# Each expert bias matmul queued behind the last product before it

## The chip, the cores and the metric

One core of one Trainium2 chip runs the program. The metric is the device time of one execution in microseconds. The kernel before took 1867.7 us (median of three executions, 1866.82 to 1869.79). The profile comes from one further execution.

## The reference

A decoder block on 512 tokens of width 1024, all float32: a mixer (a state-space branch and a pooling branch, gated), then a mixture of experts, then a final norm. What matters here is the mixture. Each token goes to 4 of 32 experts, and an expert computes

```
gu = xblk @ w_gu[e] + b_gu[e]            # 1024 -> 2048
act = glu * sigmoid(1.702 * glu) * (lin + 1)   # after clamping
out = act @ w_down[e] + b_down[e]        # 1024 -> 1024
y += out * gate                          # added to the token's row
```

## The kernel before

The mixer runs until about 713 us of the span, the mixture of experts from there to about 1850 us, and the last norm ends the program. The experts are ranked by their token counts. Those with up to 64 tokens take a *half* form: 64 rows, plain float32 products, the weights used as they were loaded. The others take a *full* form: up to 128 rows, each 1024-column piece of weights split into a high and a low part by one ScalarE (ACT) copy (L117) and one VectorE (DVE) subtraction (L118), and three products in place of one. `order_of_ranks` (L62) sets the order: one full expert, two half ones, then full and half in turn with the largest expert in the middle (it has a second block of rows), at last five full ones and two half ones.

The loop at L1351 goes over the experts. In its step u it first calls `up` for expert u (L1366), then `down` for expert u-1 (L1388). Both first call `biases`: one matmul a PSUM bank, which opens the bank's sum (`start=True`) with a row that a selector (`sel` or `wide`) picks from the bias table `bt`. `up` opens four banks of the tag "mm" for a full expert and two for a half one, `down` two or one of the tag "ss"; each tag has four banks. Then `products` adds to these banks for k = 0 to 7: L1111 to L1113 in the full form (96 matmuls in `up`, 48 in `down`), L1106 in the half form (in the trace 64 and 32 instructions on 64 columns of the array, two groups of 64 rows each). After each load of weights, hooks run: in `down` of expert u-1 they are the activation of expert u (`act_rows` from L1145, `act_turn` with transposes at L1066 from L1154), the selector of expert u+1 (`select`, L1268, GpSimd (POOL): L1273 and for half experts L1276), and the transposes that turn the rows of expert u+1 (L1082). `prep` of expert u+2 (slots, L1038 and L1039, gather L1052, gates L1059) hangs on the first k of `up`. After `down`, `send` scales the result (L1171 on ACT, L1172 on POOL) and adds it to its rows by a scattered DMA (L1175).

The order in which an engine issues is not the program's order: a planner lays the instructions out, engine by engine, when the kernel is built, by data dependences and by the times at which it thinks operands are ready. An instruction that it thinks ready can be put ahead of earlier ones of the program. On the chip each engine then follows its list. Weights are loaded on the SP queue (L771), 1 MB each, twelve an expert, into a ring of buffers, each load as soon as its buffer has been read.

Of the kernel before, what the change touches and what calls it, by code (L numbers as in the profile page):

```python
# [1 line left out]

# [1 line left out]

# [64 lines left out]
def hybrid_block(ctx: ExitStack, tc: tile.TileContext, cst, cols, rows, xt, xf, wad0, wada, bada,  # L69
                 wx, wz, wdt, wu, wg, wso, wpl, wpo, wo, wr, ball, wgu, wdn, out):  # L70
    nc = tc.nc
    V, S, G, TE, SP = nc.vector, nc.scalar, nc.gpsimd, nc.tensor, nc.sync
# [9 lines left out]
    def T_(tag, cols_, dt=F32, parts=P):  # L82
        if tag in shared:
            o = shared[tag]
            return Z[0:parts, o:o + cols_]
        uid[0] += 1
        return sb.tile([parts, cols_], dt, tag=tag, name=f"{tag}_{uid[0]}")

    def bank(tag="mm"):
        uid[0] += 1  # L90
        return pm.tile([P, 512], F32, tag=tag, name=f"{tag}_{uid[0]}")
# [21 lines left out]
    def tt(out_, in0, in1, op):  # L113
        V.tensor_tensor(out_, in0, in1, op=op)
# [369 lines left out]
    for jj in range(4):  # L484
        whi, wlo = load_split(wpo[jj])
        for i in range(2):
            j = jj * 2 + i
            ps = bank("mm")
# [254 lines left out]
    def weights(e):  # L743
        def of(w, lo_, hi_):
            return w[e, lo_:hi_, :] if isinstance(e, int) else w[bass.ds(e, 1), lo_:hi_, :].squeeze(0)

        return dict(wu=lambda k: of(wgu, k * P, (k + 1) * P), got={},
                    wd=lambda c: of(wdn, c * 256, (c + 1) * 256).rearrange("(k p) d -> p k d", p=P))
# [5 lines left out]
    def weights_of(u):  # L754
        if u not in wts:
            wts[u] = weights(order[u] if u < FIXED else
                             SP.value_load(rk["eidi"][0:1, order[u]:order[u] + 1], min_val=0, max_val=NE - 1))
        return wts[u]
# [87 lines left out]
    for n in range(2):  # L846
# [6 lines left out]
        for b in range(NB):  # L853
            ps = bank("mm")
# [163 lines left out]
    def op_of(rot, half):  # L1018
        return Op(rot(512) if half else rot(2048, F32R), half)
# [5 lines left out]
    def slots(i, pos, n_, xe):  # L1025
        half = n_ <= 64
        s4 = T_(("a2", "wrt")[i % 2 if i != "x" else 0], 4 * P, BF16)
        for b in range(NB):
            o = s4[:, b * P:(b + 1) * P]
            if half:  # L1030
                V.tensor_scalar(o.rearrange("p (h m) -> p h m", h=2), iota1[:, 0:64].unsqueeze(1).to_broadcast([P, 2, 64]),
                                pos(b), None, op0=ALU.is_equal)
            else:
                V.tensor_scalar(o, iota1, pos(b), None, op0=ALU.is_equal)
        ps = bank("ss")
        for b in range(NB):
            sb_ = s4[:, b * P:(b + 1) * P]
            TE.matmul(ps[:, 0:2], sb_, tokc[:, 0:2], start=b == 0, stop=False)  # L1038
            TE.matmul(ps[:, 0:2], sb_, tokc[:, 2 + 2 * b:4 + 2 * b], start=False, stop=b == NB - 1)  # L1039
        n = i if i == "x" else i % 6  # L1040
        st = dict(s4=s4, ps=ps, xe=xe, n=n, half=half, rows=P if half else min(n_, P))
        ix_ = T_(f"ixs_{n}", 2)
        stt(ix_[:, 0:1], ps[:, 1:2], cs[:, C_NP:C_NP + 1], cs[:, C_P5:C_P5 + 1], ALU.mult, ALU.add)
        tt(ix_[:, 0:1], ps[:, 0:1], ix_[:, 0:1], ALU.add)
        if half:
            stt(ix_[:, 1:2], ix_[:, 0:1], 2.0, cs[:, C_H:C_H + 1], ALU.mult, ALU.add)
        idx = T_(f"idx_{n}", 1, I32)
        V.tensor_copy(idx, ix_[:, 1:2] if half else ix_[:, 0:1])
        src, lim, xe = (h_d2, 2 * T - 1, xe[:, 0:512]) if half else (h_d, T - 1, xe)
        if i != 0:  # L1050
            n_ = st["rows"]
            G.indirect_dma_start(xe[0:n_, :], None, src, bass.IndirectOffsetOnAxis(ap=idx[0:n_, :], axis=0), bounds_check=lim, oob_is_err=False)  # L1052
        st.update(idx=idx, ixf=ix_[:, 0:1])
        return st

    def slot_gates(st, gv, ps=None):
        ps = ps or st["ps"]
        for b in range(NB):
            TE.matmul(ps[:, 2:5], st["s4"][:, b * P:(b + 1) * P], gv(b), start=b == 0, stop=b == NB - 1)  # L1059
        st["gate"] = T_(f"gate_{st['n']}", 1)  # L1060
        V.tensor_reduce(st["gate"], ps[:, 2:5], axis=AX.X, op=ALU.add)
# [27 lines left out]
    def rows_of(ps, n):  # L1089
        return ps[n // 2][n % 2 * 64:n % 2 * 64 + 64, :]  # L1090


    def biases(x, ps, sel, n0):
        for n, p in enumerate(ps):
            if x.half:
                c = n0 // 2 + n
                TE.matmul(p, sel["wide"], bt[:, c * 512:(c + 1) * 512], start=True, stop=False)
            else:
                h, c = (n0 + n) % 2, (n0 + n) // 2
                TE.matmul(p, sel["cols"][:, h:h + 1].to_broadcast([P, P]), bt[:, c * 512:(c + 1) * 512], start=True, stop=False)  # L1100

    def products(x, ps, k, hl, o, n0=0):
        stop = k == KD - 1
        if x.half:
            for i in range(2):
                TE.matmul(rows_of(ps, n0 + i), x.c[k], hl[:, o + i * 512:o + (i + 1) * 512], start=False, stop=stop)  # L1106
            return
        hi, lo = hl
        for i in range(2):
            p, h, l = ps[n0 + i], hi[i], lo[i]  # L1110
            TE.matmul(p, x.h[k], h, start=False, stop=False)  # L1111
            TE.matmul(p, x.h[k], l, start=False, stop=False)  # L1112
            TE.matmul(p, x.l[k], h, start=False, stop=stop)  # L1113

    def pieces(r, full):
        for o in (0, 1024):
# [46 lines left out]
    def acts(ps, aT):  # L1163
        h = len(ps) // 2
        return [lambda n=n: act_turn(act_rows(ps[n], ps[n + h]), aT, n) for n in range(h)]
# [54 lines left out]
    def sel_halves(out_, e):  # L1220
        stt(out_, cs[:, C_PM:C_PM + 2], e, cs[:, C_HM:C_HM + 2], ALU.is_equal, ALU.mult)


    def tabled(u):
        ev = SP.value_load(tab["eui"][0:1, u], min_val=0, max_val=NE - 1)
        ec, ub, eo, pu, gvu, gvf = (T_(n, c, d) for n, c, d in (
            ("ec", 2, F32), ("ub", 1, F32), ("eo", NE, F32), ("pu", 4, F32), ("gvu", 12, BF16), ("gvf", 12, F32)))
        V.tensor_copy(ec[:, 0:1], tab["euf"][:, u])
        V.tensor_copy(ec[:, 1:2], tab["ruf"][:, u])
        V.tensor_copy(ub, tab["ubase"][:, u])  # L1230
        V.tensor_scalar(eo, i32c, ec[:, 1:2], None, op0=ALU.is_equal)
        gvt = T_("q16", 512)
        pv = gvt[:, 0:P].rearrange("p (b e) -> p b e", b=NB)
        tt(pv, rk["pos"], eo.unsqueeze(1).to_broadcast([P, NB, NE]), ALU.mult)
        V.tensor_reduce(pu, pv, axis=AX.X, op=ALU.add)
        V.tensor_scalar(pu, pu, ub, None, op0=ALU.subtract)
        gvx = gvt[:, P:P + 384].rearrange("p (b c e) -> p b c e", b=NB, c=3)
        for b in range(NB):
            tt(gvx[:, b], GVv[:, b].rearrange("p e c -> p c e"), eo.unsqueeze(1).to_broadcast([P, 3, NE]), ALU.mult)
        V.tensor_reduce(gvf.rearrange("p (b c) -> p b c", c=3), gvx, axis=AX.X, op=ALU.add)  # L1240
        V.tensor_copy(gvu, gvf)
        eT = T_("eT", 2, F32R)
        sel_halves(eT, ec[:, 0:1])
        return dict(pos=lambda b: pu[:, b:b + 1], gv=lambda b: gvu[:, b * 3:(b + 1) * 3], sel=dict(cols=eT), **weights(ev))
# [12 lines left out]
    def sel_of(u):  # L1257
        if u < FIXED:
            return dict(cols=sel0[:, 2 * u:2 * u + 2])
        return dict(cols=sels[u % 2], wide=wides[u % 2])  # L1260
# [90 lines left out]
    for u in range(NE + 1):  # L1351
        hooks = {}
        if u < NE:
            w, sel = weights_of(u), sel_of(u)
# [71 lines left out]

    nov = nc.values_load(tab["novi"][0:1, 0:1], min_val=0, max_val=OVER - 1)
    with tc.For_i(0, nov, 1) as i:
        w = tabled(bass.ds(i, 1))
        xet = T_("S6", 2048)  # L1430
        G.memset(xet, 0.0)
        st = slots(6, w["pos"], P, xet[:, 0:D])
        slot_gates(st, w["gv"])
        x = turn(st, x_rot)
        aT = op_of(a_rot, False)
        for f in acts(up([x], w["sel"], w, {})[0], aT):
            f()
        part = spread(down([aT], w["sel"], w, {})[0], st)
        for b, n in sums:
            ps = bank("mm")  # L1440
            sT, cr = part[n]
            for r in range(2):
                TE.matmul(ps, sT[:, b * P:(b + 1) * P], cr[r], start=r == 0, stop=r == 1)
            tn = t0[b][:, n * 512:(n + 1) * 512]
            tt(tn, tn, ps, ALU.add)
        for b in range(NB):
            norm(b, o_rot(1024), [t0[b][:, n * 512:(n + 1) * 512] for n in range(2)])
# [85 lines left out]
```

## Time and profile before

| What | Value |
|---|---|
| median of three executions | 1867.7 us |
| the profiled execution's own time | 1870.85 us |
| its span in the profile | 1869.1 us |
| TensorE busy | 1788.1 us, 96% |
| DVE busy | 1213.9 us, 65% |
| ACT busy | 947.0 us, 51% |
| DMA over the span | mean 282 GB/s |

The median leaves out nothing that the profile has: the profiled execution is 3.15 us above it, and 1.75 us of its own time lie outside the span. Times in the profile are counted from the start of the span. A matmul's duration includes its way through the array, and successive ones overlap, so what a matmul costs is read from one start to the next.

### The profile page before, as it was taken

The numbers are of one execution on the slowest core, as the hardware profiler recorded it, in microseconds if no ns is written. First come the engines' busy times: TensorE is split into PE (matmuls) and PEld (weight loads), VectorE is DVE, ScalarE is ACT, GpSimd is POOL, SyncE is SP. The second block draws the span as 40 slices with busy tenths as digits, with TensorE's granted clock in tenths as the row PEclk, the third lists the DMA queues.
The fourth block names the chain that finished last, engine by engine and source line by source line (L and its number), as shares of the span: only waits on it lengthen the run. The fifth ranks groups of instructions, "written<-read, shape, count | busy, mean of one in ns | idle before, by whom it ended". The sixth has DMA issues, their size and how long they took to land. (4 is left out here: it accounts for less than half of the span.)

```text
span 1869.1 us, 23339 instructions
## 1 busy us (share of the span) xinstructions
PE 1788.1 (96%) x8353; PEld 1165.1 (62%) x8353; DVE 1213.9 (65%) x1803; ACT 947.0 (51%) x1458; POOL 220.0 (12%) x214
## 2 busy tenths in 40 slices
PE   6999999999999999999999999999999999999995
PEld 3787687867768777456456455455564565677741
DVE  5888685857574548657557566375675585799933
ACT  4433545536362346346455455264555455577822
POOL 0000000010100002121111111121112111211111
PEclk9999999999999999999999999999999999999998
DMA  8265233352443458999999998789999999989894
GB/s 349 76 251 221 90 135 113 113 134 93 124 130 136 178 218 296 371 402 400 388 373 402 380 366 326 305 309 373 382 402 377 380 403 364 397 327 341 316 365 191
DMA packets 102728, 527.81 MB, mean 282 GB/s; under 512 B 11737, under 2 KB 12377, under 8 KB 60368
## 3 DMA queue, kind: packets, MB, share of 16 engines
q1 hardware_dynamic: 90544, 498.14, 68.8%
q0 software_dynamic: 11184, 25.50, 6.4%
q10 hardware_dynamic: 880, 2.64, 0.4%
q8 instruction: 67, 1.10, 0.2%
q14 instruction: 53, 0.43, 0.1%
HBM read 502.89 MB, written 25.77 MB: 283 GB/s over the span
## 5 line engine op out<-in xcount | busy, mean ns | idle before, releaser
L118 DVE TENSOR_TENSOR wl<-r,wh 128x1024 fp32r<-128x1024 f32 x246 | 303.6, 1260 | 109.4 <-ACT wh L117 100.2
L117 ACT ACTIVATE wh<-r 128x1024 fp32r<-128x1024 f32 x246 | 253.9, 1057 | 136.3 <-PE mm L266 56.2
L118 DVE TENSOR_TENSOR wl<-S,wh 128x1024 fp32r<-128x1024 f32 x186 | 229.8, 1271 | 34.3 <-ACT wh L117 34.1
L1112 PE MATMUL mm<-wl,S 128*128 128x512 f32 x540 | 217.3, 402 | 9.7 <-DVE wl L118 9.0
L1113 PE MATMUL mm<-wh,S 128*128 128x512 f32 x540 | 214.5, 397 | 0.0
L117 ACT ACTIVATE wh<-S 128x1024 fp32r<-128x1024 f32 x186 | 189.5, 1055 | 47.5 <-PE mm L1113 34.9
L265 PE MATMUL mm<-S,wh 128*128 128x512 f32 x512 | 207.9, 407 | 4.0 <-ACT S L117 4.0
L267 PE MATMUL mm<-S,wl 128*128 128x512 f32 x512 | 206.3, 403 | 1.5 <-DVE wl L118 1.5
L266 PE MATMUL mm<-S,wh 128*128 128x512 f32 x512 | 206.5, 403 | 0.0
L1111 PE MATMUL mm<-wh,S 128*128 128x512 f32 x540 | 177.7, 402 | 8.0 <-ACT wh L117 8.0
L1147 DVE TENSOR_SCALAR q<-mm 128x512 f32<-128x512 f32 x49 | 32.9, 687 | 181.8 <-PE mm L1106 153.1
L1148 ACT ACTIVATE q<-q 128x512 f32<-128x512 f32 x50 | 31.3, 632 | 218.0 <-DVE q L1147 217.8
L1112 PEld LDWEIGHTS mm<-wl,S 128*128 128x128 f32 x540 | 102.2, 189 | 47.6 <-DVE wl L118 17.0
L1111 PEld LDWEIGHTS mm<-wh,S 128*128 128x128 f32 x540 | 100.6, 188 | 48.7 <-ACT wh L117 16.3
L265 PEld LDWEIGHTS mm<-S,wh 128*128 128x128 f32 x512 | 97.2, 190 | 33.0 <-issue 7.1
L1113 PEld LDWEIGHTS mm<-wh,S 128*128 128x128 f32 x540 | 102.4, 190 | 21.5
L267 PEld LDWEIGHTS mm<-S,wl 128*128 128x128 f32 x512 | 97.0, 190 | 29.7 <-issue 6.4
L266 PEld LDWEIGHTS mm<-S,wh 128*128 128x128 f32 x512 | 97.3, 190 | 26.9 <-issue 4.2
L1112 PE MATMUL ss<-wl,S 128*128 128x512 f32 x240 | 97.1, 405 | 1.9 <-DVE wl L118 1.5
L1106 PE MATMUL mm<-S,S 128*64 128x512 f32 x408 | 96.2, 596 | 0.0
L1172 POOL TENSOR_TENSOR y<-y,q 128x512 f32<-128x512 f32 x47 | 67.7, 1453 | 237.9 <-ACT y L1171 237.2
L1113 PE MATMUL ss<-wh,S 128*128 128x512 f32 x240 | 95.5, 398 | 0.0
(499 smaller groups left out, 3101.2 us busy)
## 6 DMA issues: line engine op xcount, KB each, us to landing
S<-in_wgu SPq DMA_DIRECT2D x113, 1024.0 KB, 9.6
r<-in_wgu SPq DMA_DIRECT2D x97, 1024.0 KB, 8.4
S<-in_wdn SPq DMA_DIRECT2D x61, 1024.0 KB, 11.7
r<-in_wdn SPq DMA_DIRECT2D x44, 1024.0 KB, 13.2
bc<-in_wgu SPq DMA_DIRECT2D x23, 1024.0 KB, 10.3
Z<-in_wgu SPq DMA_DIRECT2D x23, 1024.0 KB, 10.0
r<-in_wada SPq DMA_DIRECT2D x16, 1024.0 KB, 6.7
r<-in_wx SPq DMA_DIRECT2D x12, 1024.0 KB, 6.1
```

The lines of the kernel that those rows point to most:

```text
L117: S.activation(hi, src, AF.Copy)
L118: V.tensor_tensor(lo, src, hi.bitcast(F32), op=ALU.subtract)
L265: TE.matmul(ps, a, hh(k), start=k == 0, stop=False)
L266: TE.matmul(ps, a, hl(k), start=False, stop=False)
L267: TE.matmul(ps, b, hh(k), start=False, stop=k == KD - 1)
L1106: TE.matmul(rows_of(ps, n0 + i), x.c[k], hl[:, o + i * 512:o + (i + 1) * 512], start=False, stop=stop)
L1111: TE.matmul(p, x.h[k], h, start=False, stop=False)
L1112: TE.matmul(p, x.h[k], l, start=False, stop=False)
L1113: TE.matmul(p, x.l[k], h, start=False, stop=stop)
L1147: V.tensor_scalar(g, pg, LIM, None, op0=ALU.min)
L1148: S.activation(t, g, AF.Tanh, scale=ALPHA / 2)
L1172: G.tensor_tensor(yn, yn, gaf2[0] if half else gaf[n], op=ALU.mult)
```

## The change

`products` remembers its last matmul in `lastp`. `biases` issues its matmuls under `tc.issue_after`, which queues them behind that matmul in TensorE's order; it adds no wait for a result. The matmul remembered is the last one that stands before the biases in the program: for `up` of expert u+1 it is the last product of `down` of expert u-1, and for `down` of expert u-1 it is the last product of `up` of expert u. The first expert's `up` has none. The loop at the end for experts with more tokens than their room forgets it first.

```
+    lastp = []
+
     def biases(x, ps, sel, n0):
+        with tc.issue_after(lastp[0]) if lastp else nullcontext():
+            bias_rows(x, ps, sel, n0)
+
+    def bias_rows(x, ps, sel, n0):
         for n, p in enumerate(ps):
...
         if x.half:
             for i in range(2):
-                TE.matmul(rows_of(ps, n0 + i), x.c[k], hl[:, o + i * 512:o + (i + 1) * 512], start=False, stop=stop)
+                lastp[:] = [TE.matmul(rows_of(ps, n0 + i), x.c[k], hl[:, o + i * 512:o + (i + 1) * 512], start=False, stop=stop).ins]
             return
...
-            TE.matmul(p, x.l[k], h, start=False, stop=stop)
+            lastp[:] = [TE.matmul(p, x.l[k], h, start=False, stop=stop).ins]
...
     with tc.For_i(0, nov, 1) as i:
+        lastp.clear()
         w = tabled(bass.ds(i, 1))
```

## Rows read from the trace of the kernel before

**Rows 1.** The page's first part: busy us, share of the span, instructions.
```profile
PE 1788.1 (96%) x8353; PEld 1165.1 (62%) x8353; DVE 1213.9 (65%) x1803; ACT 947.0 (51%) x1458; POOL 220.0 (12%) x214
```

**Rows 2.** Stretches: length; PE, PEld, DVE, ACT, POOL busy; PEclk, DMA share, GB/s.
```profile
923.20:991.10 67.90, 65.15 (x301) 37.93 (x299) 42.23 (x58) 36.03 (x51) 10.82 (x10) 1.00 0.98 382
991.10:1060.40 69.30, 66.56 (x299) 39.07 (x297) 42.34 (x58) 36.02 (x51) 10.82 (x10) 0.98 0.99 382
1684.40:1724.60 40.20, 38.33 (x179) 29.65 (x178) 37.36 (x42) 31.50 (x40) 8.40 (x5) 1.00 0.89 331
```

**Rows 3.** TensorE's waits at full heads, 923 to 991 us: total, times, longest.
```profile
PE mm L1112 <- DVE wl L118: 0.8, 1, 0.8
PE mm L1111 <- ACT wh L117: 0.7, 2, 0.5
```

**Rows 4.** Timeline around the start of a half expert's up: start, us, instruction.
```profile
901.54 0.72 PE L1100 MATMUL ss<-bt,sel 128*128 128x512 f32 x2
902.10 0.27 PE L1066 MATMUL mm<-cst,S 128*128 128x128 f32 x1
...
905.05 0.48 PE L1100 MATMUL mm<-bt,sel 128*128 128x512 f32 x1
905.46 1.94 PE L1106 MATMUL mm<-S,S 128*64 128x512 f32 x8
...
907.43 0.49 PE L1100 MATMUL mm<-bt,sel 128*128 128x512 f32 x1
...
907.85 5.37 PE L1106 MATMUL mm<-r,S 128*64 128x512 f32 x24
```

**Rows 5.** Timeline of TensorE where the next full expert's products begin to overlap.
```profile
958.30 1.07 PE L1106 MATMUL ss<-S,r 128*64 128x512 f32 x2
959.30 0.50 PE L1112 MATMUL mm<-wl,S 128*128 128x512 f32 x1
...
960.41 1.93 PE L1106 MATMUL ss<-S,r 128*64 128x512 f32 x6
962.28 0.55 PE L1066 MATMUL mm<-cst,S 128*128 128x128 f32 x3
```

**Rows 6.** Timeline at the end of a half expert's up.
```profile
920.02 0.50 PE L1100 MATMUL mm<-bt,sel 128*128 128x512 f32 x1
920.88 0.50 PE L1100 MATMUL mm<-bt,sel 128*128 128x512 f32 x1 [0.36 <-DVE q L1149]
922.21 0.55 PE L1066 MATMUL ss<-cst,q 128*128 128x128 f32 x3 [0.82 <-DVE q L111]
```

**Rows 7.** Timeline of all engines at the head of a full expert's up.
```profile
934.42 1.27 ACT L1171 ACTIVATE y<-ss,gate 128x512 f32<-128x512 f32 x2 [2.73 <-PE ss L1113]
934.64 0.62 PE L1111 MATMUL mm<-wh,S 128*128 128x512 f32 x2
...
936.67 3.34 DVE L118 TENSOR_TENSOR wl<-r,wh 128x1024 fp32r<-128x1024 f32 x2 [2.83 <-ACT wh L117]
...
938.93 0.50 PE L1112 MATMUL mm<-wl,S 128*128 128x512 f32 x1 [0.80 <-DVE wl L118]
```

**Rows 8.** One bias of a half expert's down among full products.
```profile
926.38 0.48 PE L1097 MATMUL ss<-bt,sw 128*128 128x512 f32 x1
926.69 0.40 PE L1112 MATMUL ss<-wl,S 128*128 128x512 f32 x1
926.92 0.40 PE L1113 MATMUL ss<-wh,S 128*128 128x512 f32 x1
```

**Rows 9.** Waits of TensorE (1240 to 1300 us) and POOL; a gather on POOL.
```profile
PE ss L1059 <- DVE ixs L114: 2.0, 1, 2.0
POOL sw L1276 <- DMA S<-h_d,idx: 63.9, 8, 19.0
...
925.72 1.35 POOL L1052 DMA_INDIRECT S<-h_d,idx  x1 [16.82 <-DVE idx L1048]
```

**Rows 10.** Ten microseconds at the highest DMA rate of a pair.
```profile
915.00:925.00 10.00, 8.82 (x47) 4.18 (x44) 5.43 (x10) 4.16 (x6) 0.00 (x0) 1.00 1.01 426
```

More of the change, by code (lines that the diff above doesn't have):

```diff
@@ L1 @@
-from contextlib import ExitStack
+from contextlib import ExitStack, nullcontext
 import numpy as np
```

## The prediction

> **What bounds the kernel now.** The page's first part comes first: TensorE is busy for 96% of the span, the next engine, DVE, for 65% [rows 1]. Then the table by stretch, since the mixture of experts is where the change acts. In the middle a full and a half expert take turns, and such a pair lasts 67.9 us with TensorE busy for 65.15 and DVE for 42.23 [rows 2]: TensorE sets the pace, and only 2.75 us of a pair are left as its waits. DMA is as full there, share 0.98, but TensorE's waits name DVE and ACT, not a transfer [rows 3, 6]. The late full experts differ: 40.2 us each, DVE busy for 37.36 of them [rows 2], so DVE is nearly the bound. Last the timeline, to see where the biases stand. None of them carries much work, 0.2 to 0.4 us from one start to the next; what counts is whether TensorE had something else to do at that place.
>
> **The change, part by part.** It removes no instruction and adds none. It moves bias matmuls in TensorE's list. I follow the pair that ends near 991 us, and its neighbour at 901 us, and take what repeats.
>
> *Out of the half expert's up.* Before, the two biases of the full expert's down stand at 901.54, and 0.56 us pass to the next start [rows 4]. They belong behind the half expert's last up product, which is at 920. Two of the next full expert's four up biases stand at 905.05 and 907.43, before and inside the half expert's products: 0.41 and 0.42 us to the next product [rows 4]. They belong behind the last product of the full expert's down, at 934.6. No wait is marked beside the four, so this time is TensorE's own: 0.56 + 0.41 + 0.42 = 1.39 us go.
>
> *Into the wait for the activation.* At 920 TensorE has run out of products: from 920.02 to 922.21 it does two more up biases and then waits for the activation that the first transpose needs, 0.36 and 0.82 us marked as waits [rows 6]. The two leave for 934.6, and the two of the full expert's down come from 901.54. The same work lies in the same wait, whose end DVE sets: 0. If the planner put them elsewhere, this would cost 0.56.
>
> *To the head of the full expert's up.* All four up biases now stand between the last product of down and the first of up, near 934.6. Four starts at 0.23 us, the step in a run of full products, 926.69 to 926.92 [rows 8], are 0.93 us. In the same place TensorE waits today for the split of the second piece of weights: 0.7 for ACT and 0.8 for DVE [rows 3]. That chain hangs on the last product of down, through `send` on ACT at 934.42 and a DVE pass that begins at 936.67, and releases TensorE at 938.93 [rows 7]. Later first products then eat waiting time, so I cost the four at 0, with 0.6 us of wait left. If the cover were gone, they cost 0.93 a pair.
>
> *The half expert's down behind the full expert's up.* Its one bias moves from 926.38, where it takes 0.31 us [rows 8], to the change from full to half products; a bias there costs no more than 0.4 by the single ones [rows 4], so 0. But half products need their bias, so none can now be issued before the last full one. Before, two of them are put ahead of the last four full products: 1.00 us for the two, 1.11 for the four, 1.87 for the other six [rows 5]. In one run eight take at most 1.94 [rows 4] and four full ones 0.92 [rows 8]. 3.98 - 2.86 = 1.12 us go.
>
> A pair so gains 1.39 + 1.12 = 2.5 us. The pattern of the moved biases [rows 4] stands in ten places, from 832 to 1617 us with the largest expert's own left out, that of the split groups [rows 5] in nine pairs and once more before the last half experts: 10 x 2.5 = 25 us.
>
> *What is lost.* (a) The two biases at 901.54 stand between the slot matmuls and the gate matmuls, which wait for a short DVE chain, and may cover it; then part of their 0.56 us stays as a wait. I take 0.2 of it, ten times: 2 us. (b) The largest expert has six biases at a head where half products already fill the waits: 6 x 0.23 = 1.4. (c) In the four stretches between late full experts DVE is nearly full [rows 2], so biases among down's products cost nothing before, and at up's head they cost up to 0.93, less the waits there; I take 0.3 each, 1.2. (d) The last two half experts, about 0.5. Together 5, and 25 - 5 = 20 us.
>
> *Selectors.* A bias reads a selector that POOL may overwrite only behind the down bias of two experts earlier. That bias is now about 18 us later for a full expert, at 920 in place of 901.54. `select` then has from about 921 to 934.6 before the next up bias needs it, against a short POOL instruction: 0. The bounds are the rival below.
>
> *Loads.* No transfer's issue waits for a bias. Buffers are freed with the products, so loads come earlier as products do. At 67.9 us and 382 GB/s a pair moves 25.9 MB; in 65.5 us that is 396 GB/s, and ten microseconds of a pair ran at 426 [rows 10]. The Trainium skill, Perfetto Trace Analysis, section Roofline, gives the 16 DMA engines of a single active core about 435 GB/s in all; by that a pair's transfers could be done in 59.6 us, as an estimate, and would never bind. No run here shows that rate held for a pair. By the share of 0.98 alone they would be at their end now; that case is the first rival.
>
> *The clock.* One pair lasts 69.3 us with a mean granted clock of 0.98 [rows 2], so part of it ran at 1.2 GHz, after waits at a full expert's head. Fuller heads might save such a fall, and a longer wait elsewhere might cause one, 1.4 us each way. I count none.
>
> The sum stands against the profiled execution, 1870.85 us, which gives 1851. The runs' median is 3.15 us lower and nothing in the argument hangs on that difference, so the forecast is 1867.7 - 20 = 1848 us.
>
> **Rivals.** *Transfers cap the gain.* If a share of 0.98 is all that DMA can give, a pair cannot go below 0.98 x 67.9 = 66.5 us, and 10 x 1.4 = 14 us is the most: 1854 us. For it: the share. Against: the 426 GB/s [rows 10], and no wait of TensorE for a load in the pair.
>
> *The planner fills the vacated places again.* Half products stand with biases between them because the planner thought TensorE idle there; it may put something else in, transposes or gate matmuls, which then wait on the chip for DVE. One such wait of 2.0 us is in the trace [rows 9]. Once in each pair it takes 10 x 2.0 = 20 us, the whole gain: 1868 us. For it: the orders are laid out anew. Against: those instructions exist anyway and had the same chance before.
>
> *The selector comes too late (slower).* POOL works its list in order, and `select` is now free to go only from 921 on. If it is put behind the gather issued at 925.72, it inherits the wait for that gather: 63.9 us in eight times, a mean of 8.0 and at most 19.0 [rows 9]. It decides where that wait exceeds 934.6 - 925.7 = 8.9 us. With 13 us, between mean and longest, the full expert's head comes 4 us late; 0.6 of it lies in the wait left there, so 3.4 a pair, 34 us in all, against the 20 gained: 1882 us. For it: POOL already waits there. Against: the planner sees this dependence and can put `select` ahead of the gather, which isn't issued until 5 us after 921; POOL sits idle for 16.82 us before it [rows 9].
>
> *The change doesn't reorder.* The planner could have the biases there for other reasons; but a queued-behind edge is obeyed, and the biases at 901, 905 and 907 stand ahead of products that they must now follow. I give this nothing of its own; its time would be about 1868 us.
>
> **How the numbers follow.** The forecast 0.58, transfers 0.17, refilled places 0.14, selector 0.11. The forecast's own range is 1841 (25 us and one clock fall of 1.4 saved) to 1856 (1.7 us a pair, less the 5). A change under 0.2%, 3.7 us, is what a measurement of this kernel cannot tell from none. Faster holds the first two and 0.01 of the refilled case, 0.76; same is the rest of that, 0.13; slower is the selector, 0.11. The range of 8 in 10 goes from 1840, all of the 25 us and two clock falls, to 1868, and leaves out the selector's case and little else.
>
> **What would show it.** In the trace after: no bias between two half products of one expert; two "ss" biases right behind the half expert's last up product and the wait for DVE L111 behind them; four "mm" biases in a row at a full expert's head, with the wait for DVE L118 there down from 0.8 to 0.6 or less and that for ACT nearly gone; eight half products in one run where two and six stood. A pair of 65 to 66 us. It is wrong if pairs stay near 68 us, if TensorE waits for loads or for POOL, or if the late full experts take over 41 us.

## The result and the profile after

The changed kernel took 1837.33 us (median of four executions, 1836.64 to 1839.30) beside 1868.1 us for the kernel before (1866.82 to 1869.79, four). The ratio is 0.9835, 95% interval 0.9822 to 0.9849: 30.8 us less. Forecast were 1848 us, 20 less, and a range from 1840 to 1868. The direction was right and the gain half again as large. Two executions among those reported below took far longer than the rest, 5289.77 us of `full_down` and 3144.4 us of the kernel before beside it: the ratios leave them out, the medians given there (1853.2 and 1870.0) hold them, and without them these are 1850.54 and 1869.25.

The page's first part after, in the form of [rows 1]:

```profile
PE 1754.0 (96%) x8352; PEld 1161.8 (63%) x8353; DVE 1210.0 (66%) x1803; ACT 947.1 (52%) x1458; POOL 237.5 (13%) x214
```

TensorE does the same work in 34 us less busy time, DVE and ACT keep theirs. The gain isn't waiting that went, for its idle time is 81.0 us before and 81.5 after: the same matmuls stand closer, and fewer of them ran at the lower clock. Here are stretches with the columns of [rows 2]. First comes a pair of the kernel before, from the end of one full expert's up to the next:

```profile
892.58:960.49 67.91, 65.17 (x299) 37.93 (x301) 42.22 (x58) 36.03 (x51) 10.84 (x10) 1.00 1.01 393
```

Then the same pair after, and a late full expert after:

```profile
883.76:949.86 66.10, 63.23 (x298) 38.21 (x297) 42.09 (x58) 36.04 (x51) 11.69 (x10) 1.00 1.02 403
...
1651.88:1691.94 40.06, 38.03 (x180) 29.86 (x179) 37.62 (x42) 31.88 (x41) 9.06 (x5) 1.00 0.90 332
```

A pair is 1.8 us shorter. Late experts are as long as they were, 40.06 us for 40.20 [rows 2]. Now the two heads. Here is the timeline of TensorE behind the half expert's last up product. The line numbers behind the edit are seven higher, so L1107 is a bias, L1118 to L1120 a full product, L1113 a half one:

```profile
910.60 0.74 PE L1107 MATMUL ss<-bt,sel 128*128 128x512 f32 x2
912.88 0.52 PE L1066 MATMUL ss<-cst,q 128*128 128x128 f32 x3 [1.54 <-DVE q L111]
913.15 0.71 PE L1118 MATMUL ss<-wh,S 128*128 128x512 f32 x2
```

The two biases of the full expert's down are there, and the waits of 0.36 and 0.82 us with two biases between them [rows 6] are now one of 1.54. From the last half product to the first transpose it was 2.12 us and is 2.21. The timeline of all engines at the full expert's up:

```profile
925.00 1.27 ACT L1178 ACTIVATE y<-ss,gate 128x512 f32<-128x512 f32 x2 [2.71 <-PE ss L1120]
925.22 1.09 PE L1107 MATMUL mm<-bt,sel 128*128 128x512 f32 x4
...
927.25 3.31 DVE L118 TENSOR_TENSOR wl<-r,wh 128x1024 fp32r<-128x1024 f32 x2 [2.77 <-ACT wh L117]
...
929.47 0.50 PE L1119 MATMUL mm<-wl,S 128*128 128x512 f32 x1 [0.76 <-DVE wl L118]
```

Four biases in a row, one wait left, ACT's gone. 4.25 us pass from the first bias to the end of the wait, where 4.29 passed from the first product before [rows 7]: the four cost next to nothing, as costed. At the change to half products, and at the next slots:

```profile
949.70 0.39 PE L1104 MATMUL ss<-bt,sw 128*128 128x512 f32 x1
950.02 1.94 PE L1113 MATMUL ss<-S,r 128*64 128x512 f32 x8
951.88 0.33 PE L1066 MATMUL mm<-cst,S 128*128 128x128 f32 x1
```

```profile
959.24 0.24 PE L1059 MATMUL ss<-GV,a 128*128 128x3 bf16 x4 [0.50 <-DVE ixs L114]
```

Eight half products stand in one run where two and six stood [rows 5], and the gate matmuls wait 0.50 us for DVE, a wait that the same pair before doesn't have.

To find the rest I matched the end of each expert's up product in both traces. In the mixer, whose order is the same, the profile after is already 4.5 us ahead, some 3 of them at two falls of the clock (416 and 519 us) that only the profile before has. From 740 us on the profile after gains 29.7 us. Falls of the clock account for 3.8 of it: the profile before has three in the experts, at 1007, 1621 and 1799 us, and the profile after none. At 1007 the step gains 1.47 more than its neighbours; the other two, 0.93 and about 1.4, come from the same steps in profiles further down that do and don't have the fall. The order's 25.9 us: 1.0 in the first experts, 9.5 in the pairs before the largest expert and 10.8 in those behind it, **4.05 around the largest expert** (165.80 us to 161.75), 0.3 in the late full ones, 0.2 at the end.

### The profile page after: what moved, and what is told of

It is laid out like the page before. It is cut to its first block, busy times and chain, and to the rows that moved or that the text cites. A ratio compares the mean times of both kernels' runs of the same rounds, so it can differ in the third digit from the quotient of the medians.

```text
span 1835.5 us, 23325 instructions
## 1 busy us (share of the span) xinstructions
PE 1754.0 (96%) x8352; PEld 1161.8 (63%) x8353; DVE 1210.0 (66%) x1803; ACT 947.1 (52%) x1458; POOL 237.5 (13%) x214
## 5 line engine op out<-in xcount | busy, mean ns | idle before, releaser
L1120 PE MATMUL mm<-wh,S 128*128 128x512 f32 x540 | 213.0, 394 | 0.0
L1118 PE MATMUL mm<-wh,S 128*128 128x512 f32 x540 | 182.1, 400 | 1.9 <-ACT wh L117 1.4
L1118 PEld LDWEIGHTS mm<-wh,S 128*128 128x128 f32 x540 | 101.1, 188 | 39.3 <-issue 9.7
L1120 PEld LDWEIGHTS mm<-wh,S 128*128 128x128 f32 x540 | 101.4, 188 | 21.8
L1120 PE MATMUL ss<-wh,S 128*128 128x512 f32 x240 | 94.8, 395 | 0.0
L1113 PE MATMUL mm<-S,S 128*64 128x512 f32 x408 | 94.5, 595 | 0.0
L1179 POOL TENSOR_TENSOR y<-y,q 128x512 f32<-128x512 f32 x47 | 63.7, 1367 | 209.7 <-ACT y L1178 209.7
```

The source lines that it names most:

```text
L1113: lastp[:] = [TE.matmul(rows_of(ps, n0 + i), x.c[k], hl[:, o + i * 512:o + (i + 1) * 512], start=False, stop=stop).ins]
L1120: lastp[:] = [TE.matmul(p, x.l[k], h, start=False, stop=stop).ins]
L1179: G.tensor_tensor(yn, yn, gaf2[0] if half else gaf[n], op=ALU.mult)
```

## The experiments

Each run is timed against the kernel before on the same chip.

**One set of biases at a time.** One line of the change, its condition, is varied; the first two queue the biases of `up` or of `down` alone, the third those of the half experts' `down` alone:

```
-        with tc.issue_after(lastp[0]) if lastp else nullcontext():
+        with tc.issue_after(lastp[0]) if lastp and n0 == 0 else nullcontext():             # up_only
+        with tc.issue_after(lastp[0]) if lastp and n0 == 4 else nullcontext():             # down_only
+        with tc.issue_after(lastp[0]) if lastp and n0 == 4 and x.half else nullcontext():  # half_down
```

> Only the biases of up are queued behind the last product; those of down are free as before. Theory (each bias counts by its place): two up biases leave the half products in ten places, 0.41 + 0.42 us each, so about 8 us of the 30.8 gained: 1860 us; two half products still stand ahead of the last four full ones in nine pairs. Rival (the planner lays everything out anew, and the gain isn't tied to a place): all of the 30 us or none, 1838 or 1868.

> Only the biases of down are queued behind the last product. Theory by place: 0.56 us in ten places and the split groups of half products at 1.12 us in ten places, 17 us in all: 1851 us. Up biases still stand inside the half products. Rival (not tied to a place): 1838 or 1868.

> Only the one bias of a half expert's down is queued behind the last full product. Theory by place: no half product stands ahead of the last full ones any more, 1.1 us in ten places: 1857 us, and the first group of eight half products behind a full up stands in one run. Rival (the split costs nothing, since TensorE would wait there for the split of weights anyway): 1868 us with a wait of about 1 us in its place.

Measured beside 1871.89 us: up_only 1863.17, ratio 0.9962 (0.9949 to 0.9975), 7 less by the ratio; down_only 1849.57, 0.9881 (0.9865 to 0.9897), 22 less; half_down 1881.26, **1.0060** (1.0046 to 1.0074), 11 more. The first two add up to the whole, 29 us beside 28 to 31. The third was slower than either theory had it. TensorE and then ACT in half_down, inside the half expert's up:

```profile
909.20 1.94 PE L1113 MATMUL mm<-S,S 128*64 128x512 f32 x8
911.07 0.50 PE L1107 MATMUL mm<-bt,sel 128*128 128x512 f32 x1
913.80 0.50 PE L1107 MATMUL mm<-bt,sel 128*128 128x512 f32 x1 [2.23 <-ACT q L1074]
```

```profile
909.26 1.50 ACT L1074 ACTIVATE q<-mm,colf 128x128 f32<-128x128 f32 x4
...
912.24 1.50 ACT L1074 ACTIVATE q<-mm,colf 128x128 f32<-128x128 f32 x4 [0.82 <-DVE S L118]
```

With the half experts' down biases gone, the planner laid out the free biases anew. The two up biases that had eight half products between them [rows 4] now follow one another, and the second needs a bank that ACT is still emptying of transposes; L1074's second pass ends at 913.74. Eight such waits are 18.1 us in this profile, more than the 11 us lost. So the second rival of the prediction (the planner lays out anew, and what it puts there waits on the chip) is a real case, at 2.2 us a pair. The full change leaves only the first expert's up biases free and doesn't meet it.

**The counterpart, and the change again.** `n0 == 4 and not x.half` queues the full experts' down biases alone; the changed kernel ran beside it.

> Queued are the down biases of the full experts alone: the counterpart of half_down, which lost 9.4 us (the two full up biases came one right behind the other and the second waited 2.2 us for a bank that ScalarE was still reading). If the two counterparts were independent, this one would have to give -22.3 - 9.4 = about -32 us, 1840. My theory is that they are not, and that the place of the unqueued biases decides: here the four full up biases go behind the half up product as in down_only, without that wait, but the half down bias stands among full down products (0.3 us) and the half down's first group is split by four full products (0.56 us twice): 1.4 us a pair worse than down_only, 1863 to 1866, still faster than before.

> The changed kernel once more, on the chip of the four part runs, to set them beside it. Theory: of its gain of 30.8 us some 26 to 28 lie in the order on TensorE and some 3 to 4 in falls of the clock that this one profile happened not to have (none between its start and 1820 us, four in the profile before). Then the ratio over more runs is nearer 0.985 to 0.986, about 1844 us beside 1872, and its profile shows a fall or two in the experts. Rival: the falls belong to the old order (its short waits), the ratio stays at 0.9835 and the clock of the runs above that of the kernel before. Beside it, queueing off around the largest expert (1848.25) would cost 4 us if the step ends seen in the traces are all there is, and 8 to 9 if not.

Measured beside 1870.0 us: full_down 1853.2, 0.9898 (0.9871 to 0.9925), 19 less. The two counterparts aren't independent, as my theory had it, but my figure was some 10 us too slow: most of what `down` gives, 19 of 22 us, hangs on the full experts' two biases. They drag the four up biases along unasked. In down_only too these stand right behind the two, and there they meet the selector, the wait of the third rival:

```profile
923.57 0.73 PE L1107 MATMUL ss<-bt,sel 128*128 128x512 f32 x2
925.08 1.20 PE L1107 MATMUL mm<-bt,sel 128*128 128x512 f32 x4 [0.78 <-POOL sel L1280]
```

`again` took 1844.02 us, ratio 0.985 (0.9823 to 0.9877), 26 to 28 less, as expected for an order worth 26 and a clock that changes from run to run. Its profile repeats the steps of the first one within some hundredths of a microsecond wherever neither fell, and has one fall in the experts, at the step where the kernel before had its second. (The expectation counts four falls in the profile before up to 1820 us; there are five, two in the mixer and three in the experts.) The two ratios' intervals overlap; 26 us of order is what both profiles show.

**The largest expert.** Queueing is off in its step and the next one.

```
+        with tc.issue_after(lastp[0]) if lastp and not near[0] else nullcontext():
...
+        near[0] = u in (big, big + 1)
```

> The change as it is, but without the queueing in the two steps around the largest expert (its up, the down before it, its own down and the up behind it). My term for it: six biases uncovered at its head cost 1.4 us, so without them 1836 us. Rival: around the largest expert too biases stood among half products, and the 3 us that the two traces differ there come from the change: 1840 us.

Measured 1848.25 beside 1871.89, 0.9881 (0.9864 to 0.9898). My term (b) wanted it faster than the change. It is slower, clear of the change's first interval (0.9822 to 0.9849), while the interval of `again` (0.9823 to 0.9877) still meets it at its edge; the step ends decide. The three step ends around that expert, -0.95, -1.74 and -0.41 us in the changed kernel, are +0.27, 0.00 and -0.01 here: queueing gains 3.4 us there. By the ratios it is 5.8 beside `again`, with a rest that the two intervals cover. TensorE before, in the largest expert's neighbourhood, and after at the same work:

```profile
1209.70 0.50 PE L1100 MATMUL ss<-bt,sel 128*128 128x512 f32 x1
1210.14 1.94 PE L1106 MATMUL mm<-r,S 128*64 128x512 f32 x8
1212.00 0.50 PE L1100 MATMUL ss<-bt,sel 128*128 128x512 f32 x1
1212.34 0.39 PE L1097 MATMUL ss<-bt,sw 128*128 128x512 f32 x1
```

```profile
1195.20 0.74 PE L1107 MATMUL ss<-bt,sel 128*128 128x512 f32 x2
1195.77 0.39 PE L1104 MATMUL ss<-bt,sw 128*128 128x512 f32 x1
1196.01 0.82 PE L1066 MATMUL mm<-cst,S 128*128 128x128 f32 x6
```

A bias alone between half products goes (0.44 us), and the biases stand three in a row. The larger part is in the half products that stand between full ones. First a group of two before, then the head and a group of four after, each with the next start:

```profile
1147.21 1.07 PE L1106 MATMUL ss<-r,b 128*64 128x512 f32 x2
1148.21 0.18 PE L1038 MATMUL ss<-tokc,wrt 128*128 128x2 bf16 x1
```

```profile
1124.38 1.09 PE L1107 MATMUL mm<-bt,sel 128*128 128x512 f32 x4
1125.31 0.62 PE L1104 MATMUL ss<-bt,sw 128*128 128x512 f32 x2
1125.77 0.40 PE L1118 MATMUL mm<-wh,S 128*128 128x512 f32 x1
...
1127.25 1.08 PE L1113 MATMUL ss<-r,b 128*64 128x512 f32 x4
1128.26 0.49 PE L1118 MATMUL mm<-wh,S 128*128 128x512 f32 x1
```

A group takes 1.00 us to the next start if it holds two half products and 1.01 if it holds four. In the stretch of the largest expert's up these half products stand in 17 groups before, four of them of two, and in 15 after, all of four; in that of its down it is nine before and eight after. `no_big` has the groups of before, 17 and nine. Three groups fewer are worth 3.0 us by these rows. The gate waits there add up to 2.0 us in all three profiles and give nothing.

**The wait that is left.** The 1.54 us for the activated rows are now the longest wait of a pair (19.1 us in the profile: eleven of 1.54 to 1.56, two shorter). `qturn` queues these transposes behind the full down product's first 12; `qturn_qg` does the same to the gate matmuls also.

```
     def act_turn(l, aT, n):
-        pt = turn_tile(l)
+        with tc.issue_after(lastp[0]) if lastp else nullcontext():
+            pt = turn_tile(l)
```

> On top of the change, the transposes of the activated rows (act_turn) are queued behind the last product that precedes them in the program too: behind the first 12 products of the full down product, where the changed kernel has them ahead of it and waits 1.54 us for VectorE's rows (13 waits, 19.1 us in all). Theory: that wait is now the largest on TensorE's path and is exposed, so 15 to 18 us go: about 1826. Rival: the wait only stood in for the next late thing (weights, their splits, the head of the full up product, which waits 0.76 us already), and 0 to 5 us go: about 1840.

> qturn with the gate matmuls queued too: in the changed kernel they wait 0.50 us for the slots' index arithmetic on VectorE (9 waits, 5.5 us in all, one of 1.5); queued they come four half products or twelve full ones later, where that is long done. Theory: another 4 us less than qturn, about 1822. Rival: between two products they cost 0.07 to 0.2 us each and the gather behind the slots is no earlier: same as qturn.

Measured beside 1870.0: qturn 1856.33, 0.9920 (0.9895 to 0.9945), **slower than the change** and than both theories; qturn_qg 1851.65, 0.9910 (0.9885 to 0.9935), not told apart from qturn. TensorE, ACT and DVE in qturn:

```profile
916.74 0.73 PE L1107 MATMUL ss<-bt,sel 128*128 128x512 f32 x2
918.36 0.72 PE L1118 MATMUL ss<-wh,S 128*128 128x512 f32 x2 [0.89 <-ACT wh L117]
920.06 0.50 PE L1119 MATMUL ss<-wl,S 128*128 128x512 f32 x1 [0.98 <-DVE wl L118]
...
922.13 0.63 PE L1119 MATMUL ss<-wl,S 128*128 128x512 f32 x1
922.55 0.63 PE L1120 MATMUL ss<-wh,S 128*128 128x512 f32 x1
```

```profile
917.27 3.89 ACT L117 ACTIVATE wh<-S 128x1024 fp32r<-128x1024 f32 x4
```

```profile
917.47 1.41 DVE L111 SCALAR_TENSOR_TENSOR q<-q,q 128x512 f32<-128x512 f32 x2
918.79 3.49 DVE L118 TENSOR_TENSOR wl<-S,wh 128x1024 fp32r<-128x1024 f32 x3
```

The wait was only the first of two. Behind it the full product's first weights were not split yet, since ACT and DVE do the activation first; it now waits in two pieces, 1.87 us in all. Most of the loss is the clock. The stretches of qturn behind that head:

```profile
914.00:925.00 11.00, 9.13 (x35) 5.24 (x32) 7.21 (x8) 4.73 (x6) 0.63 (x1) 0.84 1.01 426
...
920.87:924.27 3.40, 3.40 (x11) 2.61 (x10) 2.55 (x3) 0.28 (x1) 0.00 (x0) 0.50 1.02 426
```

Granted clock 0.50, 1.2 GHz, for 3.4 us that begin just behind the two waits. Seven of the eleven such heads of this profile have that; the mean clocks of its runs are 0.984 to 0.989, those of `again` 0.989 to 0.994. By the step ends a head with the fall is 1.8 to 2.0 us longer than in the changed kernel, one without it 0.3 to 0.5.

**Both lates at once.** If two things are late behind the half product, both have to go. `early` splits the full down product's first weights during the half up product, while ACT waits 9.1 and DVE 7.6 us for work there:

```
+            early = split_early.pop(0) if split_early else None
+            r = None if early else eload(w, "wd", c)
+            for k2, (o, hl) in enumerate(early or pieces(r, not aTs[0].half)):
...
+                pre.setdefault(5, []).append(lambda: split_early.append(list(pieces(eload(weights_of(prev[0]), "wd", 0), True))))
```

> The change, and the first weights of the full down product are split during the half up product ahead of it, where ScalarE and VectorE sit idle for 9.1 and 7.6 us; the transposes stay where they are. Theory from qturn (where the full down product, let in first, waited 0.89 us for ScalarE's half and 0.98 us for VectorE's half of that split): behind the half up product two things are late at once, the rows to turn (1.54 us) and the split, and each hides the other. Taking one away alone gives nothing: 1842 to 1846, a ratio of 0.985 to 0.987 as the changed kernel. Rival: VectorE and ScalarE, freed of the split, bring the rows 1 us earlier: 1832 to 1836.

> Both taken away: the early split, and the transposes behind the first 12 products of the full down product. Theory: no wait of over 0.3 us is left behind the half up product (11 places, 1.5 us each), TensorE goes straight on, and the falls of its clock that began 1 to 3.6 us behind such waits in qturn (7 in the experts) are gone too: 14 to 17 us less than the changed kernel, ratio 0.976 to 0.978, 1826 to 1830 beside 1871. Rival: the pair is then 64.5 us long and moves the same bytes, over 400 GB/s; the weights come late, or the split does again, and the ratio stays at 0.983 to 0.986.

> early_qturn with the gate matmuls queued too, which in the changed kernel wait 0.50 us for index arithmetic (5.5 us in all). Beside each other, qturn_qg gave 0 to 4 us on qturn. Theory: 3 to 4 us less than early_qturn, 1823 to 1826. Rival: no change beside early_qturn within 1.5 us.

Measured beside 1870.26 us: early **1820.97**, 0.9737 (0.9717 to 0.9756); early_qturn 1823.3, 0.9740 (0.9716 to 0.9764); early_qturn_qg 1819.73, 0.9722 (0.9696 to 0.9748). All three beat both kernels and are not told apart. My expectation for `early` alone failed for a simple reason that its timeline shows: with the weights ready, the planner itself lets twelve full products go ahead of the transposes. TensorE, then ACT's early split, then the pair:

```profile
909.51 0.73 PE L1108 MATMUL ss<-bt,sel 128*128 128x512 f32 x2
910.08 0.39 PE L1119 MATMUL ss<-wh,S 128*128 128x512 f32 x1
...
912.86 0.60 PE L1067 MATMUL ss<-cst,q 128*128 128x128 f32 x4
```

```profile
900.36 1.99 ACT L117 ACTIVATE wh<-S 128x1024 fp32r<-128x1024 f32 x2
```

```profile
882.68:946.39 63.71, 63.12 (x298) 38.12 (x297) 42.43 (x58) 36.12 (x51) 11.58 (x10) 1.00 1.02 405
```

No wait stands at either head; the gate's 0.50 us is the only one of 63.71 us that TensorE's waits list. 2.39 us went, more than the 1.54: the 0.76 at the full up's head went too, since the second piece's split begins earlier there: DVE starts it 1.22 us behind the first bias (922.92), where it was 2.03 (927.25).

**The early split without the queued biases.**

> The early split alone, on the kernel before, without the queued biases. The early split took another 23 us from the changed kernel (1844 to 1821: the 1.54 us behind the half up product and the 0.76 us at the head of the full up product, some ten times each). If the two edits answer to different waits, it takes as much here: the rows' and the banks' waits behind the half up product (1.18 us) and the two at the head of the full up product (1.5 us) go, 22 to 27 us, 1844 to 1848, and the queued biases stay worth their 25. Rival: the planner fills the early weights in among half products and the biases stay where they cost, or land where a bank is still read as in half_down: 1855 to 1868, and the early split needs the queued biases.

Measured 1881.09 us beside 1869.29, **1.0065** (1.0042 to 1.0087): an edit that gains 21 to 23 us on the changed kernel (by the ratios and by the medians) loses 12 on the kernel before. The rival was right in kind and not slow enough. TensorE:

```profile
919.50 0.73 PE L1112 MATMUL ss<-wh,S 128*128 128x512 f32 x2
...
921.09 1.94 PE L1107 MATMUL mm<-r,S 128*64 128x512 f32 x8
922.96 0.50 PE L1112 MATMUL ss<-wh,S 128*128 128x512 f32 x1
...
927.29 0.50 PE L1101 MATMUL mm<-bt,sel 128*128 128x512 f32 x1 [0.36 <-DVE q L1151]
928.61 0.66 PE L1067 MATMUL ss<-cst,q 128*128 128x128 f32 x4 [0.82 <-DVE q L111]
```

A product needs its bias in the bank first. With the bias free, at 904.46, and the weights split by 914.28, the planner put twelve full products into the midst of the half product, which so ended 3.5 us later, and the waits of [rows 6] behind it stand there unchanged. A queued bias holds its whole product back. That is the same effect that put eight half products in a run.

## Why the prediction was wrong

*The bound.* Right. TensorE sets the pace, and a stretch without its waits (`early`, 63.71 us) runs at its busy time.

*Out of the half products, -1.39 a pair.* Right in kind: no bias stands there and the half stretch is 0.61 us shorter. From the 1.39 come the bias of the half down, which now stands in that stretch (0.32), and the gate wait (0.50): -0.57.

*Into the activation's wait, 0; to the full head, 0.* Right, +0.09 and -0.03. At the head the wait for DVE kept 0.76 us where 0.6 or less was forecast, but the stretch to its end is as long as it was.

*Split groups, -1.12.* Right: from the end of the wait at the full head to the last full product it was 21.17 us (938.93 to 960.10) and is 19.99 (929.47 to 949.46), -1.18. The two half products no longer stand among full ones. The eight are whole, but a transpose still splits a later group into two and six, as before.

*(a), 0.2 a pair.* Mis-sized: the wait is 0.50 with one at 1.5 us, 5.5 us in nine. The half down's bias, costed at 0, also gives 0.10 where it stood among full products. With -0.61 for the half stretch, 0.09, -0.03, -1.18 and -0.10 the pair comes to the measured -1.8. The pairs in sum gained 20.3 us, forecast 23.

*(b), +1.4. This is the step that failed.* "The largest expert has six biases at a head where half products already fill the waits" priced what the biases cost in the new place and not what their leaving the old one does. The price itself was right: the six take 1.39 us at that head (1124.38 to 1125.77). But the half products there closed up into three groups fewer, 3.0 us, and a bias of 0.44 left them. The stretch gained 4.05 us where 1.4 was to be lost, and no_big gives 3.4 of it to the queueing: a miss of about 5.

*(c), +1.2, and (d), +0.5.* Same mistake, smaller: -0.3 and -0.2. The late full experts show it best, 40.06 us for 40.2 [rows 2]: biases among products and biases at the head cost alike there, with DVE busy for 37.62 of the 40.06.

*The clock: "I count none".* This term failed too, by 3.8 us between the two profiles. Its falls are not spread at random. Every fall in the experts, in every profile here, begins within 4 us behind the start of a wait of TensorE, one of 1.2 to 2.5 us or two or three that come to as much; but not every such wait has one. The 1.54 us of the changed kernel had none behind them in two profiles, while a gate wait of 1.48 us in `early` had. So the length alone doesn't decide, and what else does is open. That the order can bring falls is shown by qturn (seven) and up_only (six, each behind 2.21 us; the mean clocks of its runs are 0.982 to 0.987, those of the kernel before beside it 0.987 to 0.992); that the change takes some away is not, with 0 and 1 in its two profiles against 3 in one of the kernel before.

Together: 20 forecast, +2.7 less in the pairs, 1.0 more in the first experts, 5.4 more from (b), 2.2 from (c) and (d) makes 25.9 for the order; the clock's share and the scatter of medians make up the 30.8. So of the 10.8 us by which the forecast missed, 5.9 are the order's and 4.9 are not. The order alone would have given about 1842 us, inside the forecast's range, where the 1844.02 of `again` lies too: that the first measurement fell below 1840 is the clock's doing as well, and whether the order or luck gave it that clock isn't shown.

*The rivals.* Transfers don't cap: a pair at 63.71 us with 405 GB/s is well below the 66.5 us that the share of 0.98 would have set. The share reads 1.02 there, so 0.98 was no measure of what is left. The Trainium skill, DMA: Bandwidth & Descriptors, Specifications, has a ceiling of 435 GB/s; the highest rate of a row here, 426, stays under it. Refilled places and late selectors didn't come in the change itself, where TensorE has no wait for POOL; both came when half of it was done, at 2.23 and 0.78 us.

## What to carry to other kernels

Price a moved instruction in both places, at every kind of place it stands: the forecast's error is the three places where only the new cost was counted. An instruction that opens a sum holds everything that adds to it, so its place decides where a whole product may start; half of such an edit can be worse than none, since what is left free gets a new place too. And before a wait is taken away, look for what is late right behind it: one of two lates gone cost 12 us, the other gained more than 20, once the biases held the products.

## What the runs showed of the hardware

Two short waits of 0.89 and 0.98 us, with 0.7 us of matmuls between them, were followed by 3.4 us at 1.2 GHz at seven of eleven heads in one profile of qturn; a full product then takes 0.42 us to the next start (922.13 to 922.55) in place of 0.23 [rows 8]. The 1.54 us of the changed kernel in one piece never were, in 22 places of two profiles.

Half products pay for being parted: among full products two take 1.00 us to the next start and four 1.01. Two and six take 1.00 and 1.87 [rows 5], 2.87 for eight, where eight in a run take 1.86 (950.02 to 951.88).
